# A token mixer's gated unit reordered: token halves, whole-row transfers, spread query loads and another queue for late stores

## The chip, the cores and the metric

The kernel runs on one core of one Trainium2 chip. The metric is the device time of one execution in microseconds (us). TensorE (PE) multiplies matrices, with its weight loads shown apart as PEld; VectorE (DVE), ScalarE (ACT) and GpSimd (POOL) work on elements; SyncE (SP) only issues transfers (DMAs). ACT and POOL issue transfers too, each from its own instruction stream, in order with its other work. "SPq", "ACTq" and "POOLq" in the profile are these issues.

## The reference, cut to what matters

One encoder layer over 1024 tokens of 1024 features, all in float32: a SwiGLU block, a mixer with two branches, another SwiGLU block, an embedding and a last norm. The change lies in the mixer:

```python
u = rms_norm(h, mix_norm[i])
z = u @ w_in[i]
q, k, v, s_in, gates = jnp.split(z, splits, axis=-1)
y_attn = neighbourhood_attention(q, k, v, na_rpb[i]) @ w_attn_out[i]     # 8 heads of 64
y_ssm = s5_branch(s_in, ...) @ w_ssm_out[i]
g_attn, g_ssm = jnp.split(jax.nn.sigmoid(gates), N_BRANCH, axis=-1)
h = h + (g_attn * y_attn + g_ssm * y_ssm) @ w_out[i]

def s5_branch(...):                      # forward and backward scans over 32 groups of 16 channels
    y = D * u + scan_forward(u) + scan_backward(u)
    y = jax.nn.gelu(y.reshape(bn, s, SSM_W))                             # 1024 tokens x 512
    y = y * jax.nn.sigmoid(y @ glu_w + glu_b)                            # the gated unit
    return y
```

## The kernel before, in words

**Arithmetic.** Features lie on the 128 partitions, tokens along the row, in tiles of 128x512 (`t` = 0 or 1 is the half of the tokens). Each float32 operand is split in two: `split` (lines 158 to 160) rounds a tile to `hi` on ACT and subtracts it on DVE to get `lo`. `mm3` (line 188) makes a product out of three matmuls. So every product needs an ACT cast and a DVE subtraction first, for both its operands. Large projections use Strassen's seven products in place of eight (`A7`, `ACC7`, `b_operand`).

**Order.** PE's instructions run in the order in which the program text makes them. ACT, DVE, POOL and SP instructions are put in order by a planner with a simulated clock, with the text's order as priority. Once planned, each engine runs its list strictly in order: an instruction that waits holds everything behind it, transfer issues included.

**Two streams in one.** The mixer's main stream is made of projections. A generator, `mixer_side` (line 1310), is the side stream: the main stream calls `tick()` after each `mm3`, and the generator goes on when the number that it last yielded has been ticked off. `drain()` runs what is left of it at once. Counted from its start, the main stream ticks 64 times in the scan-input projections, 64 times in the values, and then four times in each of 84 `items` (12 pairs of weight columns, seven products each, in the order i = 1, 2, 3, 4, 5, 0, 6). The four query/key pairs (`qk`) and two gate pairs (`g`) come first, mixed; the last six are gate pairs. At item 81 `drain()` is called (line 1602).

**The side stream** does, in this order: the norm of the second token half; injection into the scan's states (`inject`); scan steps on POOL (`scan_steps`, 128 in all, two of them issued in each attention unit); 64 attention units (8 heads `hd`, 2 row blocks `rb`, 4 column blocks `cb`) at 3 ticks each; then 16 pairs of scan output (`ssm_out`), whose results are stored to `y_d` by POOL (line 1187); then the gated unit. A unit's queries come from `q_d` with `load_q` (four transfers of 128 KB, at `cb` = 1), its keys with `load_k` (two of 256 KB). A head's loads wait until it stands in `ready`, which the main stream fills two products into the next pair (line 1562).

**The gated unit.** `y_d[m]` holds channel block `m` as 8 steps by 128 chunks: token = chunk x 8 + step. `glu_load(t)` loads steps 4t to 4t+3 for the four blocks, `glu_act(t)` applies Gelu, and `glu_half(t)` multiplies: for each of four `k` the weights (`glu_w`) and activations are split, two ticks pass, and four `mm3` follow; at the end come sigmoid, product and the store to `y2_d`. So a half here is a half of the steps, not of the tokens.

**Loads of the branches.** `load_br(t, 1)` (line 1471) reads token half `t` of all four blocks out of `y2_d`: for each partition 8 pieces of 64 columns, 256 bytes each. Both halves of the unit must have been stored for it. `load_br(t, 0)` reads attention's output from `o_d`; it uses the tag `k4`, which has two buffers for query/key tiles, gated-unit weights and branch weights alike. Nearly everything else here takes slots of one tag, `m`, with 24 buffers of 2 KB per partition (`tmp` and `tw`): weight blocks, their split halves, sums, queries, values, scan outputs, Gelu tiles.

**Gate stores.** Results of a gate pair are appended to `later` (line 1518) and issued by `s_store` (line 1549) on ACT, three `mm3` into the next product. Weight blocks are loaded on ACT as well (line 1506).

Of the kernel before, what the change touches and what calls it, by code (L numbers as in the profile page):

```python
# [16 lines left out]
P = 128  # L17
# [24 lines left out]
def encoder_block(ctx, tc, I, out):  # L42
# [79 lines left out]
    o_d = dtile("o_d", [512, SEQ])  # L122
    g_d = dtile("g_d", [16, P, SEQ])
    y_d = dtile("y_d", [4, P, L, NCH])
    y2_d = dtile("y2_d", [512, SEQ])
    f_d = dtile("f_d", [NPAIR, P, 512])
    e_d = dtile("e_d", [NPD, P, 384])

# [1071 lines left out]
        for a, s_ in enumerate(halves2):  # L1200
            nc.sync.dma_start(t[s_].bitcast(F32), k_d[hp, a, halves2[i]])

    def load_q(hd, rb):
        hp, i = hd // 2, hd % 2
        qs[hd, rb] = [tmp("q" + n, dt=F32R) for n in "hl"]
        for a in range(2):
            for s_ in halves2:
                nc.sync.dma_start(qs[hd, rb][a][s_].bitcast(F32), q_d[hp, a, halves2[i], hsl(rb)])

    def load_v(hd, cb):  # L1210
        n = 4 * KNC[cb]
# [55 lines left out]

    ygs = {}

    def glu_load(t):  # L1270
        for m in range(4):
            yt = ygs[t, m] = tmp("yt")
            nc.sync.dma_start(yt, y_d[m, :, 4 * t:4 * t + 4].rearrange("p t c -> p (t c)"))

    def glu_act(t):
        for m in range(4):
            A.activation(ygs[t, m], ygs[t, m], AF.Gelu_apprx_tanh)

    def glu_raw(k):
        raw = tmp("wgs")  # L1280
        nc.sync.dma_start(raw, I["wglu"][k])
        return raw

    def glu_w(raw):
        w = ap_.tile([P, 2, HT], F32R, tag="k4", bufs=2, name="wgl")
        split(w[:, 0], w[:, 1], raw)
        return w

    def glu_half(t, raws):
        os_ = [bank("glu") for _ in range(4)]  # L1290
        for k in range(4):
            w = glu_w(raws.pop(0))
            y = tmp("yh", dt=F32R), tmp("yl", dt=F32R)
            split(*y, ygs[t, k])
            if 4 * t + k < 6:
                raws.append(glu_raw((k + 2) % 4))
            yield 2
            for m in range(4):
                mm3(os_[m], (w[:, 0, ksl(m)], w[:, 1, ksl(m)]), y, k == 0, k == 3)
        for m in range(4):  # L1300
            sg = tmp("sg")
            A.activation(sg, os_[m], AF.Sigmoid, bias=glub[:, m:m + 1])
            V.tensor_tensor(sg, sg, ygs.pop((t, m)), ALU.mult)
            nc.scalar.dma_start(y2_d[ksl(m), hsl(t)], sg)
        yield 2

    stored, ready = set(), set()
    SO = 56
# [1 line left out]
    def mixer_side():  # L1310
# [25 lines left out]
        units = [(hd, rb, cb) for hd in range(NH) for rb in range(2) for cb in range(4)]  # L1336
        n = len(units)
        load_k(0)
        load_q(0, 0)
        for _ in range(6):  # L1340
            scan_steps(1)
            yield 2
# [3 lines left out]
        for j in range(n + 5):  # L1346
            if j < n:
                hd, rb, cb = units[j]
                b = 2 * hd + rb
                load_tab(b + cb // 2, (1, 2, 0, 0)[cb]) if cb < 3 else None  # L1350
                if cb == 1 and rb == 0:
                    load_q(hd, 1)
                if cb == 1 and rb == 1 and hd + 1 < NH:
                    while hd + 1 not in ready:
                        yield 1
                    load_q(hd + 1, 0)
                if rb == 0 and cb == 2 and hd + 1 in ready:
                    load_k(hd + 1)
                if rb == 1 and cb == 2 and hd + 1 < NH and hd + 1 not in khl:
                    load_k(hd + 1)  # L1360
                sms[j] = attn_scores(hd, rb, cb)
            if 0 <= j - 2 < n:
                pts[j - 2] = attn_turn(units[j - 2][2], sms.pop(j - 2))
            while late:
                nc.scalar.dma_start(*late.pop())
            if 0 <= j - 4 < n:
                hd, rb, cb = units[j - 4]
                if cb == 0:
                    O[hd, rb] = bank("O")
                attn_values(hd, rb, cb, O[hd, rb], *pts.pop(j - 4))  # L1370
                if rb == 1 and hd + 1 < NH:
                    load_v(hd + 1, cb)
            scan_steps(2)
            if j >= n:
                if j - n < 3:
                    lo[j - n] = ssm_load(j - n)
            yield 3
        scan_steps(NCH)
        for p in range(NPAIR + 1):
            if 3 <= p + 3 < NPAIR:  # L1380
                lo[p + 3] = ssm_load(p + 3)
            if p < NPAIR:
                so[p] = ssm_out(p, *lo.pop(p))
            if p > 0:
                so.pop(p - 1)()
            yield 1 + p % 2
        yield 3
        glu_load(0)
        raws = [glu_raw(0), glu_raw(1)]
        yield 11  # L1390
        glu_act(0)
        glu_load(1)
        yield 2
        glu_act(1)
        for t in range(2):
            yield from glu_half(t, raws)

    start(mixer_side())

# [58 lines left out]
    def load_br(t, b):  # L1458
# [12 lines left out]
        for k in range(4):  # L1471
            st = tmp("br")
            hi, lo = tx("bh"), tx("bl")
            mark["br"] = nc.sync.dma_start(st.rearrange("p (s c) -> p s c", s=L),
                                           y2_d[ksl(k)].rearrange("p (s c) -> p s c", s=L)[:, :, t * 64:(t + 1) * 64]).ins
            sv = st.rearrange("p (s c) -> p c s", s=L)
            hv, lv = (x.rearrange("p (c s) -> p c s", s=L) for x in (hi, lo))
            split(hv, lv, sv)
# [32 lines left out]
    def s_out(n, c, t, second, src):  # L1511
        kind, m = pairs[n]
        if kind == "g":
            if c == "21":
                z, src = tmp("z21"), src
                A.copy(z, src)
                src = z
            later.append((nc.scalar, g_d[2 * m + second, :, hsl(t)], src))
            return
        hi, lo = tmp("qkh", dt=F32R), tmp("qkl", dt=F32R)  # L1520
        if second:
# [436 lines left out]
```

## Time and profile before

| | |
|---|---|
| median of 3 runs | 2091.4 us (2090.44 to 2091.76) |
| profiled execution | 2089.91 us, span 2088.1 us |
| granted TensorE clock, mean | 0.996 |
| PE busy | 2053.6 us, 98% of the span |
| DVE, ACT, POOL busy | 1468.1, 1010.5, 468.4 us |
| DMA | 319.75 MB, mean 153 GB/s |

The span runs from the first to the last instruction; the execution's time is 1.8 us longer. Matmuls overlap, so a busy PE is not one at its peak. Places in the span, in us: scan-input and value projections to about 790; attention with query, key and gate projections to about 1040; scan output to about 1095; the gated unit from 1103 to 1141; branch loads and their first products from 1157. "Idle before" in a row is the time in which the engine stood still ahead of that instruction, with what ended it.

### The profile page before, as it was taken

The numbers are of one execution on the slowest core, as the hardware profiler recorded it, in microseconds if no ns is written. First come the engines' busy times: TensorE is split into PE (matmuls) and PEld (weight loads), VectorE is DVE, ScalarE is ACT, GpSimd is POOL, SyncE is SP. The second block draws the span as 40 slices with busy tenths as digits, with TensorE's granted clock in tenths as the row PEclk, the third lists the DMA queues.
The fourth block names the chain that finished last, engine by engine and source line by source line (L and its number), as shares of the span: only waits on it lengthen the run. The fifth ranks groups of instructions, "written<-read, shape, count | busy, mean of one in ns | idle before, by whom it ended". The sixth has DMA issues, their size and how long they took to land.

```text
span 2088.1 us, 28214 instructions
## 1 busy us (share of the span) xinstructions
PE 2053.6 (98%) x9518; PEld 1680.4 (80%) x9518; DVE 1468.1 (70%) x2478; ACT 1010.5 (48%) x1878; POOL 468.4 (22%) x688
## 2 busy tenths in 40 slices
PE   9999999999999998999999999999999999999998
PEld 3788888888888887887887788788888888888887
DVE  7897777667867846677645668986665665786855
ACT  6434333344445434677755545543333334445544
POOL 0037556441000508888230001000000000000000
PEclk9999999999999999999999999999999999999999
DMA  3434444475533567677585875243324238533302
GB/s 133 144 119 152 128 134 121 145 258 179 191 105 121 144 179 221 198 232 222 183 273 172 266 242 119 78 148 122 97 86 139 81 120 296 157 107 91 120 22 81
DMA packets 214512, 319.75 MB, mean 153 GB/s; under 512 B 37856, under 2 KB 81504, under 8 KB 214368
## 3 DMA queue, kind: packets, MB, share of 16 engines
q1 hardware_dynamic: 173840, 258.14, 39.2%
q10 hardware_dynamic: 36368, 52.46, 7.5%
q0 software_dynamic: 4160, 7.36, 1.6%
q8 instruction: 75, 1.23, 0.2%
q14 instruction: 69, 0.57, 0.1%
HBM read 224.01 MB, written 93.85 MB: 152 GB/s over the span
## 4 chain that ended last, share of the span: by engine, by line
PE 86%; DVE 6%; DMA 5%; ACT 2%; issue 1%; ACTq 0%; SPq 0%; DVEq 0%
PE dx L190 4%; PE dx L191 4%; PE dx L192 4%; PE gx L190 3%; PE ux L190 3%; PE ux L192 3%; PE gx L191 3%; PE gx L192 3%; PE ux L191 3%; PE dy L191 2%; PE dy L192 2%; PE dy L190 2%; DMA blk<-in_win 2%; PE uy L190 2%; PE gy L190 2%; PE uy L192 2%
## 5 line engine op out<-in xcount | busy, mean ns | idle before, releaser
L159 ACT CAST wh<-hbuf 128x512 fp32r<-128x512 f32 x280 | 173.0, 622 | 389.2 <-PE gx L191 84.6
L160 DVE TENSOR_TENSOR wl<-hbuf,wh 128x512 fp32r<-128x512 f32 x280 | 217.4, 779 | 122.9 <-ACT wh L159 120.8
L159 ACT CAST wh<-wblk 128x512 fp32r<-128x512 f32 x190 | 118.1, 622 | 187.2 <-PE dx L191 81.9
L160 DVE TENSOR_TENSOR wl<-wblk,wh 128x512 fp32r<-128x512 f32 x190 | 130.8, 691 | 50.7 <-ACT wh L159 43.2
L190 PE MATMUL dx<-ah,wh 128*128 128x512 f32 x416 | 163.5, 393 | 0.4 <-DVE hbuf L694 0.3
L192 PE MATMUL dx<-ah,wl 128*128 128x512 f32 x416 | 161.9, 389 | 0.0
L191 PE MATMUL dx<-al,wh 128*128 128x512 f32 x416 | 161.9, 389 | 0.0
L160 DVE TENSOR_TENSOR al<-araw,ah 128x512 fp32r<-128x512 f32 x154 | 106.6, 696 | 50.7 <-PE dx L191 18.3
L190 PE MATMUL gx<-xh,wh 128*128 128x512 f32 x320 | 125.0, 391 | 1.2 <-DVE c L581 1.2
L190 PE MATMUL ux<-xh,wh 128*128 128x512 f32 x320 | 125.0, 391 | 0.0
L192 PE MATMUL ux<-xh,wl 128*128 128x512 f32 x320 | 124.5, 389 | 0.0
L192 PE MATMUL gx<-xh,wl 128*128 128x512 f32 x320 | 124.5, 389 | 0.0
L191 PE MATMUL gx<-xl,wh 128*128 128x512 f32 x320 | 124.5, 389 | 0.0
L191 PE MATMUL ux<-xl,wh 128*128 128x512 f32 x320 | 124.5, 389 | 0.0
L159 ACT CAST ah<-araw 128x512 fp32r<-128x512 f32 x154 | 95.0, 620 | 46.4 <-PE dx L191 14.2
L1154 POOL TENSOR_TENSOR sc<-X,rho 128x128 f32<-128x128 f32 x128 | 82.4, 644 | 59.4 <-ACT X L1137 49.4
L190 PEld LDWEIGHTS dx<-ah,wh 128*128 128x128 f32 x416 | 78.1, 188 | 18.7 <-DVE hbuf L694 1.2
L428 DVE TENSOR_TENSOR hbuf<-hbuf 128x512 f32<-128x512 f32 x120 | 90.5, 755 | 2.1
L191 PEld LDWEIGHTS dx<-al,wh 128*128 128x128 f32 x416 | 78.1, 188 | 16.7 <-issue 0.7
L160 DVE TENSOR_TENSOR wl<-blk,wh 128x512 fp32r<-128x512 f32 x84 | 60.9, 727 | 43.4 <-ACT wh L159 42.9
L192 PEld LDWEIGHTS dx<-ah,wl 128*128 128x128 f32 x416 | 78.1, 188 | 16.2
L190 PE MATMUL px<-xh,wh 128*128 128x512 f32 x192 | 78.7, 410 | 3.4 <-ACT z L1539 2.6
(398 smaller groups left out, 5741.6 us busy)
## 6 DMA issues: line engine op xcount, KB each, us to landing
araw<-a_d SPq DMA_DIRECT2D x154, 256.0 KB
a_d<-c SPq DMA_DIRECT2D x148, 256.0 KB
wblk<-in_wd SPq DMA_DIRECT2D x88, 256.0 KB
hbuf<-in_wg SPq DMA_DIRECT2D x40, 512.0 KB
hbuf<-in_wu SPq DMA_DIRECT2D x40, 512.0 KB
blk<-in_win ACTq DMA_DIRECT2D x48, 256.0 KB
hbuf<-in_xT SPq DMA_DIRECT2D x32, 256.0 KB
h_d<-hbuf ACTq DMA_DIRECT2D x32, 256.0 KB
```

The source lines that it names most:

```text
L159: A.copy(hi, src)
L160: return eng.tensor_tensor(lo, src, hi.bitcast(F32), ALU.subtract)
L190: T.matmul(o, lhsT=wh, rhs=xh, start=first, stop=False, skip_group_check=more)
L191: T.matmul(o, lhsT=wh, rhs=xl, start=False, stop=False, skip_group_check=more)
L192: T.matmul(o, lhsT=wl, rhs=xh, start=False, stop=last, skip_group_check=more)
L428: V.tensor_tensor(b11, (b12, b22, None, None, b21)[i - 2], b11, ALU.subtract)
L1154: G.tensor_tensor(sc, both, rho4, ALU.mult)
```

## The change

Five edits, all in the mixer:

- `y2_d` becomes `[2, 4, P, HT]`: one whole tile per token half and block. Each branch load and each store moves full rows of 2 KB.
- The gated unit goes by token halves. `glu_load(m)` loads both step halves of one block, during the scan's output for the first three (`p` = 6, 10, 14); Gelu follows block by block. `glu_parts` gives the 64 chunks of a token half as two views of 4 x 64 columns, so split and product are two instructions each. The eight Gelu tiles live until the second half is done.
- `glu_prep` makes a step's operands before the products of the step ahead of it; the second half's first operands are made behind the first sigmoid.
- `load_q` loads one of `hi` and `lo` (two transfers), at `cb` = 0 and 1; the next head's keys come at `cb` = 3 in place of 2. Every eighth unit yields 4 ticks in place of 3, and the waits ahead of the gated unit are shorter.
- Gate stores that are traced after the scan's last step go to POOL's queue.

```diff
-    y2_d = dtile("y2_d", [512, SEQ])
+    y2_d = dtile("y2_d", [2, 4, P, HT])
...
-    def load_q(hd, rb):
+    def load_q(hd, rb, a):
         hp, i = hd // 2, hd % 2
-        qs[hd, rb] = [tmp("q" + n, dt=F32R) for n in "hl"]
-        for a in range(2):
-            for s_ in halves2:
-                nc.sync.dma_start(qs[hd, rb][a][s_].bitcast(F32), q_d[hp, a, halves2[i], hsl(rb)])
+        q = tmp("q" + "hl"[a], dt=F32R)
+        qs.setdefault((hd, rb), []).append(q)
+        for s_ in halves2:
+            nc.sync.dma_start(q[s_].bitcast(F32), q_d[hp, a, halves2[i], hsl(rb)])
...
+    def glu_load(m):
+        ygs[m] = [tmp("yt") for _ in range(2)]
+        for i in range(2):
+            nc.sync.dma_start(ygs[m][i], y_d[m, :, 4 * i:4 * i + 4].rearrange("p s c -> p (s c)"))
+    def glu_parts(t, m, *xs):
+        for i in range(2):
+            yield (ygs[m][i].rearrange("p (s c) -> p s c", s=4)[:, :, t * 64:(t + 1) * 64],
+                   *(x[:, i * 256:(i + 1) * 256].rearrange("p (s c) -> p s c", s=4) for x in xs))
...
+    def glu_prep(t, k, raws):
         w = ap_.tile([P, 2, HT], F32R, tag="k4", bufs=2, name="wgl")
+        split(w[:, 0], w[:, 1], raws.pop(0))
+        y = tmp("yh", dt=F32R), tmp("yl", dt=F32R)
+        for src, hi, lo in glu_parts(t, k, *y):
+            split(hi, lo, src)
+        if 4 * t + k < 6:
+            raws.append(glu_raw((k + 2) % 4))
+        return w, y
+
+    def glu(raws):
+        steps = [(t, k) for t in range(2) for k in range(4)]
+        nxt = glu_prep(0, 0, raws)
+        yield 2
+        for n, (t, k) in enumerate(steps):
+            w, y = nxt
+            if k == 0:
+                os_ = [bank("glu") for _ in range(4)]
+            if k < 3:
+                nxt = glu_prep(*steps[n + 1], raws)
             for m in range(4):
                 mm3(os_[m], (w[:, 0, ksl(m)], w[:, 1, ksl(m)]), y, k == 0, k == 3)
+            if k == 3:
+                for m in range(4):
+                    sg = tmp("sg")
+                    A.activation(sg, os_[m], AF.Sigmoid, bias=glub[:, m:m + 1])
+                    for src, o in glu_parts(t, m, sg):
+                        V.tensor_tensor(o, o, src, ALU.mult)
+                    nc.scalar.dma_start(y2_d[t, m], sg)
+                    if m == 0 and t == 0:
+                        nxt = glu_prep(1, 0, raws)
+            yield 2 + k % 2
...
-                if cb == 1 and rb == 0:
-                    load_q(hd, 1)
-                if cb == 1 and rb == 1 and hd + 1 < NH:
+                if cb < 2 and rb == 0:
+                    load_q(hd, 1, cb)
+                if cb < 2 and rb == 1 and hd + 1 < NH:
                     while hd + 1 not in ready:
                         yield 1
-                    load_q(hd + 1, 0)
-                if rb == 0 and cb == 2 and hd + 1 in ready:
+                    load_q(hd + 1, 0, cb)
+                if rb == 0 and cb == 3 and hd + 1 in ready:
                     load_k(hd + 1)
...
-            yield 3
+            yield 3 + (j % 8 == 7)
         scan_steps(NCH)
+        raws = []
         for p in range(NPAIR + 1):
...
+            if p in (6, 10, 14):
+                glu_load((p - 6) // 4)
+            if p in (10, 14):
+                glu_act((p - 10) // 4)
+            if p >= NPAIR - 1:
+                raws.append(glu_raw(p - NPAIR + 1))
             yield 1 + p % 2
+        glu_load(3)
         yield 3
-        glu_load(0)
-        raws = [glu_raw(0), glu_raw(1)]
-        yield 11
-        glu_act(0)
-        glu_load(1)
-        yield 2
-        glu_act(1)
-        for t in range(2):
-            yield from glu_half(t, raws)
+        glu_act(2)
+        yield 4
+        glu_act(3)
+        yield from glu(raws)
...
-            mark["br"] = nc.sync.dma_start(st.rearrange("p (s c) -> p s c", s=L),
-                                           y2_d[ksl(k)].rearrange("p (s c) -> p s c", s=L)[:, :, t * 64:(t + 1) * 64]).ins
+            nc.sync.dma_start(st, y2_d[t, k])
...
-            later.append((nc.scalar, g_d[2 * m + second, :, hsl(t)], src))
+            later.append((nc.gpsimd if scan["c"] >= NCH else nc.scalar, g_d[2 * m + second, :, hsl(t)], src))
```

More of the change, by code (lines that the diff above doesn't have):

```diff
@@ L1268, in encoder_block, with glu_act @@
     ygs = {}
[L1270 to L1277, printed above, removed]
+    def glu_load(m):
+        ygs[m] = [tmp("yt") for _ in range(2)]
+        for i in range(2):
+            nc.sync.dma_start(ygs[m][i], y_d[m, :, 4 * i:4 * i + 4].rearrange("p s c -> p (s c)"))
+    def glu_act(m):
+        for y in ygs[m]:
+            A.activation(y, y, AF.Gelu_apprx_tanh)
+    def glu_parts(t, m, *xs):
+        for i in range(2):
+            yield (ygs[m][i].rearrange("p (s c) -> p s c", s=4)[:, :, t * 64:(t + 1) * 64],
+                   *(x[:, i * 256:(i + 1) * 256].rearrange("p (s c) -> p s c", s=4) for x in xs))
     def glu_raw(k):
@@ L1282, in glu_raw @@
         return raw
-    def glu_w(raw):
+    def glu_prep(t, k, raws):
         w = ap_.tile([P, 2, HT], F32R, tag="k4", bufs=2, name="wgl")
[L1286 to L1296, printed above, removed]
-            yield 2
+        split(w[:, 0], w[:, 1], raws.pop(0))
[15 more added lines that the diff above has]
+                nxt = glu_prep(*steps[n + 1], raws)
             for m in range(4):
                 mm3(os_[m], (w[:, 0, ksl(m)], w[:, 1, ksl(m)]), y, k == 0, k == 3)
[L1300 to L1305, printed above, removed]
+            if k == 3:
[8 more added lines that the diff above has]
+            yield 2 + k % 2
     stored, ready = set(), set()
@@ L1338, in mixer_side @@
         load_k(0)
-        load_q(0, 0)
+        load_q(0, 0, 0)
+        load_q(0, 0, 1)
         for _ in range(6):
@@ L1385, in mixer_side @@
                 so.pop(p - 1)()
+            if p in (6, 10, 14):
[4 more added lines that the diff above has]
+                raws.append(glu_raw(p - NPAIR + 1))
             yield 1 + p % 2
+        glu_load(3)
         yield 3
-        glu_load(0)
-        raws = [glu_raw(0), glu_raw(1)]
-        yield 11
-        glu_act(0)
-        glu_load(1)
-        yield 2
-        glu_act(1)
-        for t in range(2):
-            yield from glu_half(t, raws)
+        glu_act(2)
+        yield 4
+        glu_act(3)
+        yield from glu(raws)
     start(mixer_side())
```

## The prediction

> **What bounds the kernel now.** I read the page's first part, then a table by stage, then what TensorE (PE) waited for, then the timeline around each wait. The page:
>
> ```profile
> span 2088.1 us, 28214 instructions
> PE 2053.6 (98%) x9518; PEld 1680.4 (80%) x9518; DVE 1468.1 (70%) x2478; ACT 1010.5 (48%) x1878; POOL 468.4 (22%) x688
> ```
>
> PE is busy for 2053.6 of 2088.1 us. The change adds and removes no matrix product, so it can win only idle time, 34.5 us in all, and what a lowered clock adds behind idle time. The stages that it touches, each row with its window, length, busy time of PE, PEld, DVE, ACT and POOL with counts, then granted clock, DMA share and GB/s:
>
> ```profile
> 780.00:825.00 45.00, 40.63 (x170) 32.35 (x169) 23.46 (x36) 16.85 (x33) 39.04 (x77) 0.96 0.70 208
> 825.00:1040.00 215.00, 207.79 (x1266) 179.13 (x1265) 150.93 (x378) 153.40 (x355) 154.89 (x307) 1.00 0.69 208
> ...
> 1095.00:1130.00 35.00, 32.20 (x133) 25.55 (x132) 19.05 (x30) 20.05 (x35) 0.00 (x0) 0.95 0.55 181
> 1130.00:1180.00 50.00, 46.87 (x196) 37.50 (x195) 27.82 (x39) 25.85 (x40) 0.00 (x0) 0.97 0.61 180
> 1180.00:1310.00 130.00, 130.00 (x575) 107.54 (x574) 101.11 (x162) 73.67 (x128) 14.06 (x16) 1.00 0.69 210
> ```
>
> PE idles 4.4 us before attention starts, 7.2 us in attention (215.00 less 207.79), 2.8 us in the gated unit and 3.1 us where the branches are loaded. The last row has no idle time: 575 products in 130 us are 0.226 us each, so a tick (three products) is 0.68 us and a step of the gated unit (twelve) 2.7 us. What ended the larger waits from 640 to 1330 us, as total, times and longest:
>
> ```profile
> PE pt L1244 <- ACT sm L1237: 5.6, 5, 2.6
> PE px L190 <- ACT z L1539: 2.6, 2, 2.2
> PE br L190 <- ACT bh L159: 2.1, 1, 2.1
> PE glu L190 <- ACT yh L159: 1.6, 1, 1.6
> ...
> PE glu L191 <- DVE yl L160: 1.1, 2, 0.9
> ```
>
> Every one is a wait for an operand that ScalarE (ACT) or VectorE (DVE) prepared late; PE waits for a DMA directly almost nowhere. So the question is what held ACT and DVE.
>
> **The gated unit.** Start, length, engine, line:
>
> ```profile
> 1102.64 0.69 DVE L1543 TENSOR_TENSOR z<-py,z 128x512 f32<-128x512 f32 x1 [0.68 <-PE py L192]
> ...
> 1103.37 0.33 ACTq L1549 DMA_DIRECT2D g_d<-z  x1
> 1103.75 0.63 ACT L1277 ACTIVATE yt<-yt 128x512 f32<-128x512 f32 x1 [2.51 <-DVE z L1543]
> ...
> 1104.28 0.60 ACT L159 CAST yh<-yt 128x512 fp32r<-128x512 f32 x1
> ...
> 1104.93 0.50 PE L190 MATMUL glu<-yh,wgl 128*128 128x512 f32 x1 [1.65 <-ACT yh L159]
> ...
> 1126.20 0.50 PE L191 MATMUL glu<-yl,wgl 128*128 128x512 f32 x1 [0.92 <-DVE yl L160]
> ```
>
> ACT stood idle for 2.51 us ahead of the Gelu at 1103.75. What it did just before is a gate store, issued at 1103.37, the moment the DVE addition it stores is done (1102.64 + 0.69). The store is queued on ACT in front of the Gelu and of the cast `yh`, and PE waits 1.65 us for that cast. The second half of the unit opens with another 0.92 us. A gap also lowers the clock behind it:
>
> ```profile
> 945.00:950.00 5.00, 4.51 (x26) 3.60 (x25) 3.37 (x11) 4.66 (x13) 4.22 (x11) 1.00 0.57 186
> 1105.00:1110.00 5.00, 4.77 (x13) 3.54 (x14) 2.00 (x3) 2.83 (x6) 0.00 (x0) 0.66 0.41 107
> 1165.00:1170.00 5.00, 2.67 (x7) 1.89 (x7) 2.60 (x4) 3.48 (x5) 0.00 (x0) 0.80 0.16 64
> 1170.00:1175.00 5.00, 5.00 (x20) 4.04 (x20) 5.00 (x6) 5.00 (x6) 0.00 (x0) 0.86 0.02 3
> ```
>
> At 1105 to 1110 the clock is 0.66, at 1165 to 1175 it is 0.80 and 0.86: 5.00 x 0.34 = 1.7 us and 5.00 x (0.20 + 0.14) = 1.7 us lost, each behind a gap of about 2 us. It isn't certain: behind the 2.62 us gap quoted last the clock stayed at 1.00. The Trainium skill, page "TensorE: Matmul & The Clock Gate", section "Why this matters for your kernels", says that drops are avoided as long as no gap exceeds about 3 us; the trace disagrees at two places (gaps of 1.65 and 2.10 us) and agrees at the third. By that rule the two clock terms would not hang on the gaps, and the sum below would be 5.1 instead of 8.5.
>
> Part by part: **operands a step ahead** and **token halves.** Today weights and operand of a step are split two ticks (1.4 us) ahead of its products. Afterwards the split of step n+1 is issued in front of the products of step n: 2.7 us of products and two or three ticks, 4.1 to 4.8 us. Gelu of the first tiles moves into the scan's output loop, off the unit's start. That removes the 1.65 us, the 0.2 us that is left of the 1.1 us in the wait table, and the 1.7 us of clock. The second half's first operand is now issued behind one sigmoid instead of four, but three ticks ahead instead of four; I take half of its 0.92 us away. Term A: 1.65 + 0.2 + 0.45 + 1.7 = 4.0 us; bounds 0 (all of it waits anew) and 4.5 (2.80 + 1.7). Slicing by tokens makes each split two instructions on half the columns:
>
> ```profile
> 1076.20 0.37 ACT L1184 COPY ys<-yo 128x256 f32<-128x256 f32 x1
> L159 ACT CAST yh<-yt x8: 600/620/624, 1104.3 to 1131.3; 128x512 fp32r<-128x512 f32 x8
> ```
>
> Two ACT instructions of 256 columns for one of 512 are 2 x 0.37 - 0.62 = 0.12 us more per step, about 1 us over eight steps, and I take the same for DVE. ACT is busy 20.05 of 35 us there and the step ahead covers it: nothing, and 2 us if the cover were gone. The pieces of 64 columns may cost more than a plain 256; doubled, it is still under the 2.7 us of a step.
>
> **Pacing.** One more tick after every eighth unit makes eight ticks, 5.4 us, and slows attention against the projections; the wait between the scan's output and the first gated product shrinks from 18 ticks to 9. Counted from the side generator's start, the last gated products come at tick 440 in both, and the forced drain at tick 452, so nothing is dumped late. The last Gelu tile is wanted only in the fourth step, 17 ticks and three steps (20 us) behind the last scan product. It costs nothing as long as the units aren't late for readiness of the next heads: query loads now ask one unit earlier, at ticks 211, 261 and 311, against readiness at 190, 246 and 302.
>
> **Whole-row transfers and gate stores.** The branch loads today (y_d here is the array y2_d, whose digit the profile drops):
>
> ```profile
> 1147.96 8.17 SPq L1474 DMA_DIRECT2D br<-y_d  x6
> ...
> 1155.32 0.68 DVE L1543 TENSOR_TENSOR z<-pz,z 128x512 f32<-128x512 f32 x1
> ...
> 1159.98 0.39 ACTq L1549 DMA_DIRECT2D g_d<-z  x1
> 1160.03 1.92 SPq L1464 DMA_DIRECT2D br<-o_d  x1
> ...
> 1160.40 0.59 ACT L1516 COPY z<-px 128x512 f32<-128x512 f32 x1 [6.40 <-DMA br<-y_d]
> ...
> 1166.52 9.25 ACT L159 CAST bh<-br 128x512 fp32r<-128x512 f32 x10 [3.13 <-DMA br<-o_d]
> ...
> 1167.18 0.50 PE L190 MATMUL br<-bh,wh 128*128 128x512 f32 x1 [2.10 <-ACT bh L159]
> ```
>
> Six loads that pick 64 of 128 columns per step, rows of 256 bytes, keep SP's queue for 8.17 us, 1.36 us each; a plain store is issued in 0.39. Behind them stands the last attention load, issued at 1160.03. ACT is held too: the gate store at 1159.98 had its data at 1156.00 (1155.32 + 0.68), the copy at 1160.40 comes out after 6.40 us of idleness, and the casts start when the late load lands (1166.52, 6.5 us after issue). PE waits 2.10 us. After the change each load is 128 rows of 2 KB; six issues of 0.39 instead of 1.36 free SP up to 5.8 us earlier. The load still needs a buffer of two that the weight splits hold; I count 4 us. It then lands at 1162.5, and cast and subtraction (0.6 and 0.7) are over by 1164, ahead of PE's wish at 1165.1. The first half is also loaded when its own stores are done, not when all eight are. Term B: 2.1 + 0.2 + 1.7 of clock = 4.0; I take 3.5, since the ten casts of 9.25 us behind it stay; bounds 0 and 4.8 (3.13 + 1.7).
>
> The gate stores traced after the scan, 24 of 32, go to POOL. No row shows one there; the nearest is another 256 KB store from POOL:
>
> ```profile
> L1090 POOL DMA_DIRECT2D s_d<-s x4: 559/580/792, 699.2 to 703.6; - x4
> DMA to landing us min/median/max: 2.5/3.1/3.7
> ```
>
> 24 x 0.58 = 14 us on an engine that is busy 0.00 us from 1095 to 1180, and 24 x 0.33 leave ACT with the blocking seen twice above. POOL's scan steps and the stores of the scan's output can now stand behind a gate store that waits for its sum; the output's last tile has the 20 us above. Landing takes 3.1 us, at most 3.7 in these four: nothing, bounds 0 and, if each late buffer costs one wait, the rival below. The Trainium skill, page "DMA: Bandwidth & Descriptors", section "Issuing engines are not separate DMA queues", says that issuing from several engines saves only issue time, usually small. The trace has an issue held 4 us past its data. By that rule the move itself would be worth nothing on the path, B would rest on the loads alone, and with half of it gone the sum would be 6.7.
>
> **Loads of queries and keys, spread.** Attention's worst wait:
>
> ```profile
> 933.66 1.79 SPq L1208 DMA_DIRECT2D qh<-q_d  x2
> 933.70 0.36 ACTq L1506 DMA_DIRECT2D blk<-in_win  x1
> 935.55 4.19 SPq L1208 DMA_DIRECT2D ql<-q_d  x2
> 941.54 0.85 DVE L428 TENSOR_TENSOR blk<-blk 128x512 f32<-128x512 f32 x1 [4.65 <-DMA blk<-in_win]
> 942.96 0.61 ACT L1237 ACTIVATE sm<-sm,stat 128x384 f32<-128x384 f32 x1 [6.01 <-DVE stat L1236]
> 943.62 0.55 PE L1244 MATMUL pt<-ident,sm 128*128 128x128 f32 x3 [2.62 <-ACT sm L1237]
> ```
>
> A weight block issued on ACT at 933.70 meets four query loads of one burst; it is used at 941.54, DVE stands 4.65 us for it with the reciprocal queued behind, ACT 6.01, PE 2.62. Half of the burst moves a unit away, the keys' load too. The other four waits of this kind (5.6 - 2.6 = 3.0 us) are shorter. I take term C as 1.0 us; bounds 7.2 won, or 2.6 lost (one more such wait from the new alignment). Whether the 2.62 repeats I can't tell, so C stays near zero.
>
> **Sum.** 4.0 + 3.5 + 1.0 = 8.5 us. From the profiled execution's 2089.91 (span 2088.1 plus 1.8): 2081.4. The median of the runs, 2091.4, lies 1.5 above it; carried over, **2082.9 us**.
>
> **Rivals.**
>
> *Attention smooths as well.* If bursts cause most of its waits, 6.2 of 7.2 us go instead of 1.0: 2077.7. For it: the wait above, and a slower pace. Against: the other waits are under 1.2 us and not all behind loads.
>
> *The stall moves.* PE gets past the attention operands and meets those of the gated unit, for which ten casts need 9.25 us on ACT, 0.93 each. Then B gives nothing and C is 1.0 lost: 2091.4 - 4.0 + 1.0 = 2088.4. For it: one ACT queue in order. Against: the first half's loads no longer wait for the second's stores.
>
> *The change doesn't do it.* ACT, DVE and SP are ordered by a planner; if it puts the new splits just ahead of their products again, the waits remain: 2091.4.
>
> *Slower: buffers run out.* All these tiles share 24 slots. In the gated unit today: 8 `yt`, 2 operand halves, 2 raw weights, about 6 split weights, 4 blocks and 2 sums, 24. After: two halves more, and four `yt` aren't freed at half time, because a tile now holds both token halves. That slots are short already shows here:
>
> ```profile
> 1111.62 13.07 SPq L1281 DMA_DIRECT2D wgs<-in_wglu  x4
> ```
>
> Four raw weight loads take 13.07 us to be issued. The point from which it decides: when a weight block's load, issued on ACT in order, waits for a slot, ACT stands with all casts behind it. Three such waits, for the three last gate pairs, at 2.1 + 1.7 each are 11.4; A and B lost: 2091.4 + 11.4 - 1.0 = 2101.8. Against: in the second half the last pair has no further blocks to load, and the slots of attention are free by then.
>
> **How the numbers follow.** Chances: forecast 0.55, attention smooths 0.15, stall moves 0.14, doesn't do it 0.05, slower 0.11. The forecast's own range is 2079.5 to 2086.5 (A and B at 4.5 and 4.8 with C at 2.6, or A and B halved). The range reaches to 2076 for most of the second case and to 2092 for the two without effect; it leaves out the slower case and a little below. A measurement tells 0.2%, 4.2 us, from no change: faster 0.70, same 0.19, slower 0.11.
>
> **What would show it.** After: no idle ACT ahead of the unit's first cast and PE idle under 0.8 us from 1095 to 1130 with the clock at 1.00 (A); branch loads of some 0.4 us each on SP, no gate store on ACT there, PE idle under 1 us from 1130 to 1180 (B); attention's idle between 5 and 8 us (C). It is wrong if the PE waits in these stages add up to as much as now, or if ACT's or SP's waits for slots grow.

## The result: slower by 1%, and the profile after

The changed kernel takes 2112.1 us (median of 4 runs, 2110.0 to 2113.0) against 2091.6 for the kernel before beside it (4 runs, 2090.4 to 2092.9): the ratio is 1.0096, 95% interval 1.0079 to 1.0114. The forecast was 2082.9 with a range up to 2092.0, so the time is outside it and on the other side. The profiled execution took 2112.6 us. Its page begins:

```profile
span 2110.6 us, 28252 instructions
PE 2055.1 (97%) x9518; PEld 1681.7 (80%) x9518; DVE 1468.0 (70%) x2494; ACT 1009.8 (48%) x1886; POOL 479.9 (23%) x712
...
PE 77%; POOL 9%; DVE 5%; DMA 3%; ACT 2%; issue 2%; SPq 0%; ACTq 0%; DVEq 0%
```

The span grew by 22.5 us and PE's busy time by 1.5: the loss is idle time. The last line gives each engine's share of the chain of work that ended last. POOL now has 9% of it; before the change it has none:

```profile
PE 86%; DVE 6%; DMA 5%; ACT 2%; issue 1%; ACTq 0%; SPq 0%; DVEq 0%
```

A share isn't a price: the run with the stores between the scan's steps, below, has POOL at 9% too, without the long wait of the changed kernel.

The same stages as in the prediction's table, moved along with the work; the third is the scan's output:

```profile
780.00:825.00 45.00, 41.04 (x172) 32.88 (x171) 24.30 (x37) 17.32 (x34) 38.47 (x76) 0.96 0.67 205
825.00:1062.00 237.00, 213.70 (x1274) 183.51 (x1273) 151.08 (x381) 153.61 (x357) 160.04 (x318) 0.96 0.64 192
1062.00:1118.00 56.00, 53.73 (x350) 47.93 (x350) 26.65 (x59) 32.68 (x73) 21.99 (x37) 1.00 0.85 268
1120.00:1156.00 36.00, 29.94 (x118) 23.59 (x117) 18.99 (x40) 18.98 (x40) 3.01 (x6) 0.91 0.43 140
1156.00:1205.00 49.00, 47.86 (x211) 39.31 (x210) 28.74 (x45) 25.53 (x40) 2.59 (x5) 1.00 0.58 196
1205.00:1335.00 130.00, 128.68 (x567) 105.87 (x566) 100.58 (x161) 74.60 (x128) 14.02 (x16) 1.00 0.67 205
```

Length less PE's busy time gives PE's idle time:

| stage | idle before | idle after | difference |
|---|---|---|---|
| ahead of attention | 4.4 | 4.0 | -0.4 |
| attention | 7.2 | 23.3 | +16.1 |
| scan's output | 0.1 | 2.3 | +2.2 |
| gated unit | 2.8 | 6.1 | +3.3 |
| branch loads | 3.1 | 1.1 | -2.0 |
| branch products | 0.0 | 1.3 | +1.3 |

(The 0.1 is from a window of 50 us in the scan's output of the kernel before, in which PE is busy for 49.93.) That is 20.5 of the 22.5 us; PE's longer busy time is 1.5 more. The waits of PE from 820 to 1270 us, as total, times and longest:

```profile
PE pt L1244 <- ACT sm L1237: 23.0, 8, 16.5
PE glu L190 <- ACT yh L159: 4.3, 1, 4.3
PE yo L1182 <- ACT xs L1174: 2.0, 1, 2.0
PE py L190 <- ACT z L1558: 1.8, 1, 1.8
PE br L190 <- DVE gt L1672: 1.3, 1, 1.3
```

One wait, 16.5 us long, is as large as attention's whole difference. It has no counterpart before the change, where the longest wait of this kind is 2.6 us. ACT, PE and POOL around it (start, length, engine, line, and at the end the idle time before with what ended it):

```profile
1006.70 0.62 ACT L159 CAST wh<-blk 128x512 fp32r<-128x512 f32 x1 [20.39 <-DMA g_d<-z]
...
1007.89 0.90 PE L1244 MATMUL pt<-ident,sm 128*128 128x128 f32 x3 [16.46 <-ACT sm L1237]
...
1003.62 0.32 POOL L1155 TENSOR_TENSOR sc<-sc 128x64 f32<-128x64 f32 x1
1004.02 0.32 POOL L1156 TENSOR_TENSOR X<-sc,X 128x64 f32<-128x64 f32 x1
1004.28 1.65 POOL L1568 DMA_DIRECT2D g_d<-z  x3
```

The same time in windows of 5 us, with the columns of the table by stage:

```profile
995.00:1000.00 5.00, 0.00 (x0) 0.00 (x0) 0.00 (x0) 0.00 (x0) 4.14 (x12) 0.60 0.00 1
1005.00:1010.00 5.00, 2.11 (x11) 2.02 (x12) 2.65 (x6) 3.25 (x8) 0.93 (x2) 0.50 0.53 182
1010.00:1015.00 5.00, 5.00 (x23) 4.14 (x22) 2.82 (x10) 3.31 (x8) 0.54 (x1) 0.70 0.62 184
```

A chain can be read off. ACT's cast of a weight block waits 20.39 us, and what releases it is the landing of a gate store `g_d<-z`: the cast's output needs a slot of tag `m`, and the sums `z` hold it until they are stored. The three oldest of these stores leave POOL in one burst at 1004.28, right behind its last scan step (begun at 1004.02), though ACT has stood since 986 and PE since 991. From 995 to 1000 only POOL works, and the DMAs move 1 GB/s. Behind ACT's cast stands the attention operand `sm`, for which PE waits. When PE starts again its clock is 0.50 and 0.70: 2.11 x 0.50 + 5.00 x 0.30 = 2.6 us more.

The gated unit's idle time grew by 3.3 us, where 2.3 were to go. ACT and PE at its start:

```profile
1121.02 0.36 ACT L1184 COPY ys<-yo 128x256 f32<-128x256 f32 x1
...
1128.21 1.27 ACT L1277 ACTIVATE yt<-yt 128x512 f32<-128x512 f32 x2 [3.93 <-DMA yt<-y_d]
1129.38 1.31 ACT L159 CAST yh<-yt 128x256 fp32r<-128x256 f32 x4
...
1130.13 0.80 PE L190 MATMUL glu<-yh,wgl 128*128 128x512 f32 x1 [4.31 <-ACT yh L159]
```

The Gelu at 1128.21 is that of the last block, which the products want only in the fourth step. But in ACT's list it stands ahead of the casts of the first, so ACT waits 3.93 us for the last block's load and PE 4.31.

The branch loads went as hoped. Six of them now take SP 3.31 us where they took 8.17, and PE's idle time there is down:

```profile
1173.22 3.31 SPq L1494 DMA_DIRECT2D br<-y_d  x6
```

### The profile page after: what moved, and what is told of

Its sections match the earlier page's. It is cut to its first block, busy times and chain, and to the rows that moved or that the text cites. A ratio compares the mean times of both kernels' runs of the same rounds, so it can differ in the third digit from the quotient of the medians.

```text
span 2110.6 us, 28252 instructions
## 1 busy us (share of the span) xinstructions
PE 2055.1 (97%) x9518; PEld 1681.7 (80%) x9518; DVE 1468.0 (70%) x2494; ACT 1009.8 (48%) x1886; POOL 479.9 (23%) x712
## 4 chain that ended last, share of the span: by engine, by line
PE 77%; POOL 9%; DVE 5%; DMA 3%; ACT 2%; issue 2%; SPq 0%; ACTq 0%; DVEq 0%
PE dx L190 4%; PE dx L191 4%; PE dx L192 4%; POOL sc L1154 4%; PE gx L190 3%; PE ux L190 3%; PE ux L192 3%; PE gx L192 3%; PE gx L191 3%; PE ux L191 3%; POOL X L1156 3%; POOL sc L1155 3%; PE dy L190 2%; PE dy L191 2%; PE dy L192 2%
```

## The experiments

Ratios are to the kernel before, which took 2091.0 us (median) beside the first four rows, 2092.6 beside the second four and 2091.6 beside the last. A ratio is made from all the runs; it isn't the quotient of the two medians.

| run | median us | ratio | 95% interval |
|---|---|---|---|
| all gate stores on ACT | 2097.9 | 1.0031 | 1.0015 to 1.0047 |
| before, with only the stores on POOL | 2102.9 | 1.0059 | 1.0044 to 1.0074 |
| stores on POOL from the ninth pair | 2100.7 | 1.0044 | 1.0029 to 1.0059 |
| before, with only the loads spread | 2099.8 | 1.0044 | 1.0029 to 1.0059 |
| gated unit and branch rows alone | 2099.0 | 1.0032 | 1.0019 to 1.0045 |
| before, with only whole rows | 2096.2 | 1.0022 | 1.0009 to 1.0035 |
| gated unit and branch rows alone, two Gelus late | 2091.4 | 1.0000 | 0.9991 to 1.0010 |
| stores between the scan's steps | 2102.6 | 1.0053 | 1.0038 to 1.0068 |
| all Gelus held | 2089.9 | 0.9986 | 0.9974 to 0.9998 |
| before, one tick moved | 2094.3 | 1.0003 | 0.9991 to 1.0016 |
| all Gelus held, loads spread | 2092.4 | 0.9996 | 0.9984 to 1.0007 |
| all Gelus held, short rows | 2089.7 | 0.9986 | 0.9972 to 0.9999 |

### Is it the stores on POOL?

The theory on trial: the stores' place in POOL's list, behind the whole scan, keeps their buffers. First the changed kernel with all gate stores on ACT, as before:

```diff
-            later.append((nc.gpsimd if scan["c"] >= NCH else nc.scalar, g_d[...], src))
+            later.append((nc.scalar, g_d[...], src))
```

> The whole change, but all gate stores stay on ACT. Theory Q (the loss comes from gate stores that stand on POOL behind the scan's last step and hold their buffers): PE's 16.5 us wait near 990 us is gone and so is its clock loss; with the gains forecast for the gated unit and the branch loads the time is 2083 to 2089. Rival S (slots run out because of eight Gelu tiles and operands a step ahead): the wait stays, 2100 to 2112.

Measured: 2097.9 us, 14.1 less than with POOL (1.0031 against 1.0096). Attention's waits:

```profile
PE pt L1244 <- ACT sm L1237: 9.1, 11, 2.3
```

The long wait is gone, as theory Q says. The time isn't down to its 2083 to 2089: some 6.5 us above the kernel before stay, so the other edits don't win what they were to.

The other way round, the kernel before with nothing but the stores moved:

```diff
-            later.append((nc.scalar, g_d[...], src))
+            later.append((nc.gpsimd if scan["c"] >= NCH else nc.scalar, g_d[...], src))
```

> The kernel before with only the gate stores moved to POOL after the scan's last traced step. Theory Q: a PE wait of 12 to 20 us in attention appears, ended by an ACT cast that waits for a gate store; 2103 to 2113. Rival S: nothing of the kind, 2088 to 2094.

Measured: 2102.9 us, 1.0059. One wait of PE, the longest of four, is longer than the whole loss of 11.9 us:

```profile
PE pt L1244 <- ACT sm L1237: 16.3, 4, 14.8
```

And ACT's timeline shows what made it:

```profile
1008.43 0.59 ACT L1516 COPY z<-px 128x512 f32<-128x512 f32 x1 [16.16 <-DMA g_d<-z]
```

So this edit makes the stall without any of the others. Next, only the stores of the last four gate pairs on POOL, which are traced well behind the scan's real end:

```diff
-            later.append((nc.gpsimd if scan["c"] >= NCH else nc.scalar, g_d[...], src))
+            later.append((nc.gpsimd if n >= 8 else nc.scalar, g_d[...], src))
```

> The whole change, but POOL takes gate stores only from the ninth pair on (16 of 32), which are made after the scan's real end near 1004 us. Theory Q (place in the queue): no long wait near 990 us, within 4 us of the variant with all stores on ACT. Rival P (stores from POOL are slow in themselves or disturb others): still 6 us or more above that variant.

Measured: 2100.7 us, 1.0044; its interval and that of the run with all stores on ACT overlap. No long wait in attention is left (8.4 us in 9 waits, 2.4 at most), with 16 stores issued by POOL at 0.54 us each. So those 16 do no harm that can be told, and win nothing either.

That the place decides, not the engine, was tested by moving the place. Ahead of attention the scan is issued at half pace (one of the places is shown), and steps traced later are held behind the stores traced earlier (`mark["gs"]` is the last of them); 24 stores stay on POOL:

```diff
-            scan_steps(4)
+            scan_steps(2)
...
+            with tc.issue_after(mark["gs"]) if "gs" in mark else nullcontext():
+                G.tensor_tensor(sc, both, rho4, ALU.mult)
...
-            later.append((nc.gpsimd if scan["c"] >= NCH else nc.scalar, g_d[...], src))
+            later.append((nc.gpsimd if n >= 6 else nc.scalar, g_d[...], src))
```

> The changed kernel with the same 24 late gate stores on POOL, but the scan traced at half pace and the scan steps traced later held behind them in POOL's list, so that the first four stores stand between scan steps and no longer behind the last one. Theory Q (the stores' place behind the whole scan, with their buffers, makes the long stall near 990 us): the stall of 16 us on PE is gone or under 6 us, attention idle 9 to 13 us, 2097 to 2104. Rival P (that POOL issues them is what costs, wherever they stand): the stall stays at 12 us or more and the time at 2108 to 2114.

Measured: 2102.6 us, 1.0053, 9.5 us under the changed kernel. The stores now leave between the steps, and the stall splits:

```profile
988.09 0.58 POOL L1571 DMA_DIRECT2D g_d<-z  x1
...
992.86 0.56 POOL L1571 DMA_DIRECT2D g_d<-z  x1
...
992.65 0.62 ACT L159 CAST wh<-blk 128x512 fp32r<-128x512 f32 x1 [7.02 <-DMA g_d<-z]
...
993.84 0.55 PE L1245 MATMUL pt<-ident,sm 128*128 128x128 f32 x3 [2.63 <-ACT sm L1238]
```

ACT's longest wait for a store in attention is 7.02 us in place of 20.39 (two of 2.4 and 2.6 us follow), and the wait of PE behind it 2.63 in place of 16.46. Of the rival, that a store issued by POOL costs wherever it stands, nothing is left in attention that can be told: 10.0 us of idle time there, against 9.1 with all stores on ACT. The whole time is 4.7 us over that run's by the medians, with intervals that overlap. The wait ahead of the gated unit (4.5 us) is the one that the run with the stores on ACT has too.

### Is it the spread loads?

The kernel before with the queries' loads spread and the next keys a unit later, at the old pace:

```diff
-                if cb == 1 and rb == 0:
-                    load_q(hd, 1)
+                if cb < 2 and rb == 0:
+                    load_q(hd, 1, cb)
...
-                if rb == 0 and cb == 2 and hd + 1 in ready:
+                if rb == 0 and cb == 3 and hd + 1 in ready:
```

> The kernel before with only the query loads spread over two units and the next keys a unit later; no change of pace, gated unit or stores. By the forecast's term C: 1.0 us won, 2089 to 2093, and PE idle in attention 5 to 7 us in place of 7.2. If the bursts cause most of attention's waits: under 2087.

Measured: 2099.8 us, 1.0044, slower than either outcome written above. Attention's waits did not shrink; they came elsewhere, and two later stages lost as well:

```profile
PE pt L1244 <- ACT sm L1237: 8.3, 8, 3.9
PE br L190 <- DVE gt L1654: 2.6, 1, 2.6
PE glu L190 <- ACT yh L159: 2.4, 1, 2.4
```

Five waits of 5.6 us became eight of 8.3. Then the reverse: the changed kernel with its stores on ACT and the old query loads and pace, so that only the gated unit and the whole rows are left of the change:

```diff
-                if cb < 2 and rb == 0:
-                    load_q(hd, 1, cb)
+                if cb == 1 and rb == 0:
+                    load_q(hd, 1)
...
-            yield 3 + (j % 8 == 7)
+            yield 3
```

> The changed kernel with all gate stores issued by ACT, the old query loads and the old pace: so the kernel before with the gated unit reordered and the branch loads in whole rows, nothing else. Theory S (the spread loads are what the kernel with ACT's stores still loses, 6.3 us net): without them the attention idle goes back to about 7 us without clock loss, the branch's won 3 to 4 us stay, and the wait of about 4 us ahead of the gated unit's first product stays, so 2089 to 2094. Rival G (the gated unit's reordering loses it, through the planner's new orders): 2096 to 2100, with attention idle of 9 us or more.

Measured: 2099.0 us, 1.0032, the same as with spread loads and new pace (1.0031). So the loads aren't what that kernel lost, and neither outcome written above fits well: the time is the rival's, but attention idles 8.1 us, not over 9. The loss is found a stage later. The timeline of ACT and PE in the scan's output:

```profile
1077.77 1.28 ACT L1277 ACT_TABLE_LOAD   x1 [4.63 <-DMA yt<-y_d]
...
1080.04 1.22 PE L1182 MATMUL yo<-xs,emi 128*128 128x128 f32 x4 [4.80 <-ACT xs L1174]
```

The wait at the gated unit, in the table of PE's waits:

```profile
PE glu L190 <- ACT yh L159: 3.7, 1, 3.7
```

The Gelu of the first block, moved into the scan's output loop by the change, does there what that of the last does at the unit's start: it holds ACT for a load, 4.63 us (the wait shows at the load of its table, which ACT does just ahead of it), and the copy of the scan states that PE waits for stands behind it.

### Where the Gelu stands

The run above, with the third block's Gelu held behind the last copy of the scan's output and the fourth's behind the casts of the first step:

```diff
-        glu_act(2)
+        with tc.issue_after(mark["ys"]):
+            glu_act(2)
         yield 4
-        glu_act(3)
...
+            if n == 0:
+                with tc.issue_after(mark["cast"]):
+                    glu_act(3)
             for m in range(4):
                 mm3(os_[m], ...)
```

> The kernel of e5 with the Gelu of the third pair of tiles issued by ACT behind the last scan-output copy, and that of the fourth behind the casts of the first gated step. Theory A (ACT's Gelu waits in order for loads that wait for the last scan output, and the first cast stands behind it): the idle ahead of the first product of the gated unit falls from about 5 to 6 us to 1 or 2, and the time is 3 to 5 us under e5, 2084 to 2090. Rival: the loads of the first two pairs, or the y stores by POOL, are as late, and the wait stays: within 1.5 us of e5.

Measured: 2091.4 us, 1.0000: 7.6 less by the medians, where 3 to 5 were expected, though just above the 2084 to 2090. The wait ahead of the gated unit's first product, 3.7 us, is gone. The one in the scan's output is still there:

```profile
PE yo L1182 <- ACT xs L1174: 4.4, 1, 4.4
```

Behind it the clock falls to 0.50, by the windows:

```profile
1080.00:1085.00 5.00, 4.32 (x15) 3.93 (x16) 0.50 (x1) 3.62 (x9) 2.18 (x4) 0.50 0.48 152
```

So the first two blocks' Gelus were held too, behind the scan-output copies that are traced ahead of them:

```diff
             if p in (10, 14):
-                glu_act((p - 10) // 4)
+                with tc.issue_after(mark["ys"]):
+                    glu_act((p - 10) // 4)
```

> The kernel with the Gelu of the third and fourth pair late, and now also the Gelu of the first and second pair held behind the scan-output copies traced before them. Theory A (every early Gelu holds ACT for a load that takes 4 to 6 us to land): in the scan-output stage the wait of 4.4 us on PE for the copy of the scan states, and the 3.5 us of lost clock behind it, go; 8 us less idle and clock than in the run without it, 2083 to 2086, under the kernel before by 0.3 per cent or more. Rival: the later Gelus meet the first casts and the wait returns ahead of the gated unit, 2088 to 2093.

Measured: 2089.9 us, 0.9986 (0.9974 to 0.9998): faster than the kernel before, by 0.14%, with an interval that only just leaves out no change. The median is above the 2083 to 2086 of theory A and within the rival's range, but the wait that the rival named, ahead of the gated unit, didn't come. Gated unit and branch loads, in the prediction's windows:

```profile
1095.00:1130.00 35.00, 34.54 (x152) 27.86 (x151) 21.39 (x44) 22.56 (x45) 1.18 (x2) 1.00 0.52 173
1130.00:1180.00 50.00, 47.54 (x210) 39.07 (x209) 32.93 (x52) 29.04 (x45) 0.00 (x0) 1.00 0.71 235
```

The three largest sums of PE's waits from 820 to 1270 us:

```profile
PE px L190 <- DVE z L1565: 2.5, 1, 2.5
PE pt L1244 <- ACT sm L1237: 2.4, 4, 1.6
PE s L1228 <- DMA ql<-q_d: 1.0, 2, 0.7
```

The wait of 4.4 us is gone, with the clock behind it. The profiled execution's span, 2085.8 us, is 8.6 under that of the run without it, as expected. The runs' medians differ by 1.5 only, and this kernel's executions lie between 2082.5 and 2094.9: a profile is one draw out of these. That the wait goes with the Gelu's place is shown by the traces; that it is worth 8 us in the mean isn't.

Spread loads and new pace on top of it (the changed kernel, stores on ACT, all Gelus held):

> The changed kernel with all gate stores on ACT and all Gelus held: the run with held Gelus plus the spread loads and the new pace. Theory C (the spread loads and the pace win about 1 us, as forecast): 1 us under that run, 2082 to 2086. Rival S (they add idle time and lost clock in attention, as they did on the kernel before): 2 to 8 us over it, 2086 to 2093.

Measured: 2092.4 us, 0.9996, against 0.9986 without: 2 us more by the ratios, with intervals that overlap. In its profile attention idles 8.8 us against 4.2. No gain, and no loss that can be told.

### Do the short rows make the branches late?

The kernel before with whole-row branch loads and nothing else; the gated unit still goes by steps, so each of its stores is split in two:

```diff
-            nc.scalar.dma_start(y2_d[ksl(m), hsl(t)], sg)
+            for h_ in range(2):
+                nc.scalar.dma_start(y2_d[h_, m]...[:, 4 * t:4 * t + 4], sg...[:, :, h_ * 64:(h_ + 1) * 64])
...
-            nc.sync.dma_start(st..., y2_d[ksl(k)]...[:, :, t * 64:(t + 1) * 64])
+            nc.sync.dma_start(st, y2_d[t, k])
```

> The kernel before with only the branch loads in whole rows; each store of the gated unit is split into two pieces of 64 columns. Theory B (the branch stage's waits come from loads in short rows): the branch stage's idle and lost clock fall from 4.2 us to 1.5 or less, the rest stays, 2086 to 2089. Rival: the waits come from the gate loads beside them or from the order, and stay: 2090 to 2093; the doubled stores of short pieces could hold ACT in the gated unit and cost 1 to 2 us on top.

Measured: 2096.2 us, 1.0022, above both outcomes. SP's issues are as short as hoped, and PE waits all the same, now for a gate:

```profile
1160.73 3.17 SPq L1476 DMA_DIRECT2D br<-y_d  x5
...
1194.37 0.50 PE L190 MATMUL br<-bh,whh 128*128 128x512 f32 x1 [2.66 <-DVE gt L1654]
...
1128.50 3.46 ACTq L1305 DMA_DIRECT2D y_d<-sg  x6
```

The last line is the price on the other side: six split stores hold ACT's queue for 3.46 us in the gated unit, in which PE idles 3.5 us against 1.2 in the kernel before. The cleaner test is the kernel with held Gelus and only the rows made short again, in the stores and in the loads; PE's order is the same in both:

```diff
-    y2_d = dtile("y2_d", [2, 4, P, HT])
+    y2_d = dtile("y2_d", [512, SEQ])
...
-                    nc.scalar.dma_start(y2_d[t, m], sg)
+                    nc.scalar.dma_start(y2_d[ksl(m)]...[:, :, t * 64:(t + 1) * 64], sg...)
```

> The run with held Gelus, but the gated unit's result again in rows of the whole sequence, so that its stores and the branch loads both move pieces of 256 bytes; PE's order is the same in both. Theory B (the loads in short rows make the branch stage's waits): branch idle and lost clock of 3 to 5 us instead of 0, so 3 to 5 us over that run. Rival (the branch stage is helped by the gated unit's new order alone): within 1 us of it.

Measured: 2089.7 us, 0.9986, the same as with whole rows. SP is slow again:

```profile
1152.84 7.43 SPq L1497 DMA_DIRECT2D br<-y_d  x6
```

And PE doesn't wait, by the window over the branch stage's start:

```profile
1165.00:1215.00 50.00, 50.00 (x223) 41.32 (x222) 35.41 (x51) 32.73 (x50) 0.00 (x0) 1.00 0.94 334
```

So the rows' length alone isn't it. Between the branch stage's first and last product PE idles 2.4 to 4.8 us in all five kernels whose gated unit goes by steps (before, stores moved, loads spread, rows alone, one tick), and 0.0 to 1.3 us in seven of the nine that have it by token halves; the other two have 2.1 and 2.9. What in the reordered unit does it wasn't separated. In part the wait is only moved: between the unit's last product and the first of the branches PE idles 2.5 to 2.8 us in three of these seven, against 0.8 before the change.

### What a new order alone is worth

Every edit makes the planner order ACT, DVE and SP anew. The kernel before with one tick more ahead of the injections, and no other difference:

```diff
-        yield 7
+        yield 8
         new_x()
```

> The kernel before with one tick more of delay ahead of the scan's injections; no work is added or removed. PE's order differs in 49 lines, ACT's in 364. It measures what a new order alone is worth. Theory L (a few us of the small variants' loss are the order's): the time moves by 2 to 6 us, with attention idle and lost clock of 9 to 12 us instead of 7. Rival: within 1.5 us of before, and then the losses of the spread loads (8 us) and of the whole rows alone (4 us) are their own.

Measured: 2094.3 us, 2.6 more by the medians, but with a ratio of 1.0003, which isn't told from no change; attention idles 7.3 us, as before. So the theory that small variants lose some us by a new order alone isn't borne out by this one. The interval of the spread loads (from 1.0029 on) lies above this run's (up to 1.0016); that of the rows alone (from 1.0009 on) overlaps it, so their loss can't be told from a new order's. One edit of this kind doesn't bound what others might do.

## Why the prediction was wrong

**The gate stores: the step that failed.** The sum held nothing for the move of the gate stores to POOL, and it cost 12 to 14 us. "An engine that is busy 0.00 us from 1095 to 1180" was right, and the wrong window. The first of the moved stores belong to the time around 985, and the profile of before has both halves of the answer, the ACT stores and POOL's last scan step:

```profile
983.09 0.33 ACTq L1549 DMA_DIRECT2D g_d<-z  x1
...
995.39 0.35 ACTq L1549 DMA_DIRECT2D g_d<-z  x1
...
1003.55 0.32 POOL L1156 TENSOR_TENSOR X<-sc,X 128x64 f32<-128x64 f32 x1
```

Four gate stores (983 to 995) leave ACT while POOL is in its chain of scan steps, until 1003.87. "Traced after the scan's last step" is a place in the program text. When the text's later parts are already running on the other engines, POOL is still at its scan steps, and what is put behind them waits for their end. The first store would have been 1003.9 - 983.1 = 20.8 us late; ACT's wait in the run is 20.39. The prediction did look at the order between scan and stores, but only one way round: scan steps that stand behind a store. The durations were right (0.58 us an issue taken, 0.54 measured; landing 3.1 taken, 3.5 in the middle, though 7.0 at most and not 3.7); the place wasn't looked up. Priced by the run with only this edit, it costs some 12 us, and 14 in the changed kernel.

The Trainium skill, page "DMA: Bandwidth & Descriptors", section "Issuing engines are not separate DMA queues", says that starting transfers on several engines saves no more than the time to start them. The runs agree as far as the gain goes: 16 late stores moved to POOL win nothing (2100.7 against 2097.9 us). The 12 us that the move lost come from the place in the new engine's list and not from the issuing.

**The slower rival** had the right resource, the 24 slots, and the wrong place: it let them run out in the gated unit by new tiles, at 11.4 us, and they ran out in attention by sums that weren't stored. Its 2101.8 is 10 us low: the stall cost 12 to 14 us and not 11.4, and term A, which it counted as lost, turned into a loss of its own. The deciding wait it named, ACT in order behind something that needs a slot, is what happened.

**Term A** (4.0 us): the gated unit's new order wins most of what was said once nothing stands in front of it. In the run with all Gelus held PE idles 0.46 us from 1095 to 1130 at a clock of 1.00, against 2.80 at 0.95: 2.3 + 1.7. The two later profiles with all Gelus held have 1.8 us of idle time from the scan's last output product to the unit's last, where the kernel before has the 2.8, and a clock of 1.00: 1.0 + 1.7. Which of the unit's edits does it wasn't separated. The step that failed here is "The last Gelu tile is wanted only in the fourth step, 17 ticks and three steps (20 us) behind the last scan product", from which the Gelu's new place was put at no cost. When a tile is wanted doesn't matter to an engine that runs in order; what counts is which instructions stand behind the one that waits. The Gelu stood ahead of the first cast, and the first block's ahead of the copy of the scan states. Undoing both brought the time from 2099.0 to 2089.9, more than the whole term.

**Term B** (3.5 us): the size is nearly right for the place, by luck, since the reason is wrong. SP's issues shrank as worked out, to 0.55 us each by the reckoning that gave 1.36 before and 0.40 in the middle of the eight, where 0.39 was expected; the idle time fell from 3.1 to 1.1 us there, though 1.3 came in the branch products. But with short rows back the wait stays away, and with whole rows alone it stays. That gate stores left ACT isn't it either, since with all of them on ACT PE idles 0.0 us in the branch products. What is left is the gated unit's new order, in a way that stays open.

**Term C** (1.0 us): not there. Lost, 9 us on the kernel before at the old pace; 0 and 2 us, neither told from nothing, in the two comparisons within the changed kernel. Breaking up the burst that made the worst wait only moved the waits: eight of 8.3 us for five of 5.6. The bound of 2.6 us lost was too near.

**Why the mended kernel is no better than 0.14%.** In the profile of the run with all Gelus held, gated unit and branches won what A and B said (stages here go by PE's first and last product of each): 4.6 us of idle time and clock became 0.5 in the unit, 4.2 became 0.0 in the branch products. New waits took most of it back: 2.2 us in the scan's output where there were 0.1, 2.5 between unit and branches (the `px` line above) where there were 0.8, and some 2.4 more ahead of attention. Attention's idle time was 3.0 us shorter, but with a clock of 0.99 for 1.00, and the program's start idled 1.1 more; these about cancel. 8.3 won less 6.2 is 2; the profiled spans differ by 2.3 and the runs by about 3. "The stall moves" had been a rival with 0.14, and in the small it is what is left of the change once its two faults are mended.

## What to carry to other kernels

Before work is moved to an idle engine, look up what that engine does at the time of each moved instruction, the first one above all, and not only in the stage that the change is about; "traced after" is no time. A store holds its buffer until it lands, so a store put behind a long chain can stop every engine that takes buffers of the same tag. On an engine that runs in order, an instruction whose input comes late has to stand behind everything that is wanted before that input arrives, however late its own result is wanted.

## What the runs showed of the hardware beyond what was expected

- The clock fell with PE's gap, but behind short gaps only at times. Behind the gap of 16.46 us it was 0.50 when PE came back and 0.70 in the next 5 us; behind one of 4.42 us 0.50; behind one of 2.63 us, in the run with the stores between scan steps, 1.00 over the 20 us around it; behind one of 2.5 us, in the run with all Gelus held, 1.00 over the 50 us quoted. The Trainium skill, page "TensorE: Matmul & The Clock Gate", section "Why this matters for your kernels", puts the limit at gaps of about 3 us. The 14 profiles, from 680 to 1270 us, agree above it: behind each of 12 gaps of 3.0 us and more the clock was 0.50 or 0.51 in the first 2.5 us. Below it they don't: of 65 gaps of 1.5 to 3 us, 34 were followed by a lowered clock. The plainest case is a gap of 1.9 to 2.2 us near 796 us, ahead of attention, that all 14 have: behind it the clock was lowered in six (in the kernel before to 0.66 over 5 us, which is 1.7 us lost) and stayed at 1.00 in eight. So clock terms such as the 1.7 us in A and in B are chances and not fixed costs, and a comparison of two single profiles carries such draws.
- Loads of the scan's output for the gated unit land late: in the run with two Gelus late, the first pair was issued from 1072.41 to 1073.20 and released ACT at 1078.41, 5.2 us after the second issue.
- One kernel's executions spread more than the first medians suggested: 2082.5 to 2094.9 us for the one with held Gelus, and 2087.7 to 2100.7 for the kernel before. At 12 and 35 runs the interval is still 0.24% wide, more than the 0.14% that is left of the change.
